# First block, layer 1: tokens kept in the order of their phases from the normalized rows on

## The chip, the cores and the metric

The kernel runs on one core of a Trainium2 chip. The metric is device time in microseconds (us) of one launch, the median of several runs. A core has TensorE (PE in the profile; PEld is its loading of stationary operands, "weight loads" below), VectorE (DVE), ScalarE (ACT), GpSimd (POOL) and SyncE (SP), which in this kernel issues nearly all the transfers (DMAs). Each engine works through its own instructions in order and waits for others by semaphores.

## What is computed

Two transformer-like blocks stand one after the other, each of two layers, on 512 tokens of 1024 features. The change touches only layer 1 of the first block, a dilated attention with six heads of 128 features and three groups:

```
DIL_GROUPS = ((128, 1), (512, 4), (2048, 16))      # (window, dilation)
...
for g, (window, dil) in enumerate(DIL_GROUPS):
    qkv = (h @ w_in[:, base:base + 3 * MIXER_WIDTH]).reshape(B, T, 3, DIL_HEADS, DIL_HEAD_DIM)
    q = partial_rope(qkv[:, :, 0], pos)
    k = partial_rope(qkv[:, :, 1], pos)
    o, lse = dilated_group(q, k, qkv[:, :, 2], window, dil)
```

With dilation 4 a token attends only to tokens of the same remainder by four, its phase; with dilation 16 to those of the same remainder by sixteen, which lie in the same phase too. Group 0 (dilation 1) needs neighbours of all phases. The outputs of the groups are mixed by a softmax over their log-sum-exps; an attention to a small memory, a gate, and `x + branch @ w_out` follow.

## The kernel before

All of `x`, features and weights are 4-byte numbers. A dense product is made exact enough by splitting both operands in two parts, hi and lo, and adding three products (hi hi, hi lo, lo hi). The normalized tokens stand feature-major in the two tiles `hTh` and `hTl`, [128 features, 8, 512 tokens].

`wsplit` (L269) brings a weight unit: a DMA of 512 KB (384 KB for units 384 wide) into `raw` (2 buffers), ACT copies it to `hi`, DVE writes `lo` (4 buffers each). `mm_a_g` (L293) makes a product with features on the partitions: the weights are stationary, 512 tokens stream, 24 products to a unit. `mm_b_g` (L314) makes tokens by features: 128 tokens are stationary, the weight unit streams, 24 products to a token tile.

Layer 0 ends in `w_out` (L714): for each of 4 token tiles 48 products, DVE adds the residual, `pre` (L1794) stores x to DRAM (`xd`) and normalizes, `post` transposes on PE and calls `norm_post` (L365): half of the features at a time, four transposes into `tp` (2 buffers in PSUM), four scalings into `hf`, by turns on ACT and DVE, then `split_into` (L556): ACT writes `hTh`, DVE writes `hTl`. The post of a tile comes a tile later. Before the last post, `fill.step(cols)` emits the first 12312 columns of what follows. In the kernel before that is `dil_values` (L971): the values of three heads, group 0 by token tiles (`v0`, 384 wide, 4 units), then 512 columns (`v1`, 4 units) and 256 columns (`v2`, 2 units) of groups 1 and 2 by phases. `phase_tiles` (L989) takes the stationary tokens of phase p as `xT[..., p::4]`, every fourth element.

`dil_layer` (L992) drains these products, then makes the queries and keys of head 0 (`head`, L1020, six units; `rope_fn` turns 32 rows with DVE, POOL and DVE), and goes through 24 items (6 heads by 4 phases): `front` makes the scores of the three groups in one PSUM tile `at`, `mid` transposes the weights, `back` multiplies by the values; dense products of the next head are stepped in between. In `front` group 0 (L1040) takes `q[:, 128 * a + p:128 * a + 128:4]` as stationary, groups 1 and 2 (L1044) `q[:, p::4]` against `k[:, p::4]`. `mem_stages` (L639) takes the queries `qm` by phases in the same way (L642, 8 fronts of this layer). After head 2 the values of heads 3 to 5 are made by `dil_values` again.

The order of instructions on each engine is set by a scheduler at build time, which goes by priorities and its own costs; weights get a higher priority, so their DMAs come early on SP. In the background `mod_steps` (L417) streams 512-KB rows (`bgraw`) that DVE multiplies (L425, two operations each), one step after so many dense columns.

Of the kernel before, what the change touches and what calls it, by code (L numbers as in the profile page):

```python
# [22 lines left out]
KT = 8  # L23
# [38 lines left out]
def layout(inp):  # L62
    """Rearranges the inputs into the blocks in which the chip reads them."""
# [62 lines left out]
    # the rows of the Fourier features, each beside the row of its mirror  # L126
# [14 lines left out]
def constants():  # L141
# [8 lines left out]
    c["rope1"] = np.stack([np.concatenate([cos, cos]), sn, sn * np.float32(-(128 ** -0.5))], axis=1)  # L150
    m = np.full((128, 4, 512), POS, np.float32)
    q = np.arange(128)
    for p in range(4):
        j = np.arange(256)
# [29 lines left out]
    # along the features 33 cosines and 31 sines (half of them, for the sums with the mirrored tokens); the signs  # L184
    # of a feature under mirroring, and of its mirror's row of weights
# [31 lines left out]
def pipe(items, *stages):  # L217
    """the stages of the items, each a step behind the one before"""
# [7 lines left out]
class Filler:  # L226
    """dense products, emitted a few columns at a time between the steps of a chain"""
# [21 lines left out]
class Builder:  # L249
# [42 lines left out]
    def mm_a_g(self, ps, w, xT, n0, n):  # L292
        """ps[128 features, n tokens] = w.T @ x.T in three passes; yields the columns streamed"""  # L293
# [17 lines left out]
    def mm_b_g(self, ps, xs, units, nk):  # L311
        """ps[128 tokens, n] = x @ w; xs(k) gives the stationary parts; units: [(wh, wl)] of [128, kpu, n]"""
# [36 lines left out]
    def rstd2(self, ss):  # L349
        """the same of a token's two halves"""  # L350
# [14 lines left out]
    def norm_post(self, pool, xn, a, b, dst, sl):  # L365
# [32 lines left out]
    def h_tiles(self, pool, ctx=False):  # L398
        """normed features, feature-major, in two parts: of the tokens, or of the context"""
# [8 lines left out]
    def mod_steps(self, p, todo, bufs):  # L408
        """the parts (layer, which) of the modulation: the conditions' rows times the columns of the weights"""
# [3 lines left out]
        for l, r in todo:  # L413
            # the last layer ends without the context
# [29 lines left out]
    def to_rows(self, row, src, dst):  # L444
        """feature-major columns to rows in DRAM, by way of the tile row"""
# [12 lines left out]
    def tick(self, n):  # L458
        """every so many columns of dense products, one step of the matvecs"""
# [7 lines left out]
    def pool(self, ctx, name, bufs=1, **kw):  # L467
        """a pool of tiles, on the left stack of the memory unless told otherwise"""
# [18 lines left out]
    def small_terms(self):  # L487
        """what hangs on the small inputs alone"""
# [27 lines left out]
        # lower bounds: the first layer's are the cumulative sum less itself, 0  # L516
# [22 lines left out]
        # the 0/1 masks, as the integers a predicated copy wants  # L539
# [448 lines left out]
    def phase_tiles(self, xT):  # L988
        return [(p, lambda k, p=p: (xT[0][:, k, p::4], xT[1][:, k, p::4])) for p in range(4)]  # L989
# [899 lines left out]
```

## Time and profile before

| | |
|---|---|
| median of 3 runs | 2639.84 us (2638.75 to 2646.22) |
| profiled execution, first to last instruction | 2640.8 us |
| PE busy | 2547.6 us (96%) |
| DVE busy | 1518.6 us (58%) |
| ACT busy | 1029.2 us (39%) |
| POOL busy | 174.8 us (7%) |
| mean granted TensorE clock | 0.990 of full speed |
| layer 1 of the first block (about 285 to 785 us) | PE busy 499.2 of 500 us |

A row of a timeline is: start in us, duration in us, engine, line, operation, out<-in, form, count; idle time of the engine and what ended it stand in brackets. In a form such as `128*128 128x256 f32` the first pair is the stationary operand, the second the streaming one. Matmuls are pipelined: their durations overlap, so what one costs on a busy PE is the distance from its start to the next start. Rows of one line, engine or tile give the duration as min/median/max.

### The profile page before, as it was taken

To read this page: it belongs to the slowest core of one execution; us is meant where nothing else is said; L and a number is where in the kernel's file an instruction comes from. 1 tells how busy PE (TensorE), PEld (TensorE's weight loads), DVE (VectorE), ACT (ScalarE), POOL (GpSimd) and SP (SyncE) were. 2 spreads that over 40 slices of the span, in tenths; PEclk is the share of its full clock that TensorE was granted. 3 is DMA by queue.
4 is the path that set the end of the run, shared out by engine and by line. 5 is a ranking of instruction groups with operands and counts; after the bars stand their busy time and mean duration, and the time that the engine had idled before them with its cause. 6 is when DMAs were issued, how large, how long until landed. Compare 5 with 4: busy or idle time off the path is not lost.

```text
span 2640.8 us, 38328 instructions
## 1 busy us (share of the span) xinstructions
PE 2547.6 (96%) x15539; PEld 2125.2 (80%) x15539; DVE 1518.6 (58%) x2502; ACT 1029.2 (39%) x1962; POOL 174.8 (7%) x160
## 2 busy tenths in 40 slices
PE   8999999999999999699999999999999899999998
PEld 7777987797887888577888888888788777888887
DVE  5657678635356467467666644444657676543444
ACT  5523323323345444266642212212655265622222
POOL 0000012102000010010200000000200001000001
PEclk9999999999999999899999999999999999999999
DMA  5424444222132211431544333332221343422222
GB/s 186 153 83 159 158 151 127 89 84 76 45 114 98 73 34 50 141 113 55 199 140 133 127 127 112 120 128 88 80 81 57 103 146 112 139 93 96 96 90 94
DMA packets 85680, 287.24 MB, mean 109 GB/s; under 512 B 9872, under 2 KB 10720, under 8 KB 85120
## 3 DMA queue, kind: packets, MB, share of 16 engines
q1 hardware_dynamic: 85024, 283.42, 32.4%
q8 instruction: 122, 2.00, 0.3%
q10 hardware_dynamic: 480, 1.38, 0.1%
q14 instruction: 54, 0.44, 0.1%
HBM read 257.97 MB, written 25.20 MB: 107 GB/s over the span
## 4 chain that ended last, share of the span: by engine, by line
PE 80%; DMA 5%; DVE 5%; ACT 4%; issue 3%; POOL 1%; SPq 0%; DVEq 0%; POOLq 0%; ACTq 0%
PE acc L302 13%; PE acc L298 13%; PE acc L299 13%; PE acc L318 10%; PE acc L319 10%; PE acc L320 10%; DMA qk0k<-yl 1%; ACT hi L285 1%; PE tp L1399 1%; DVE lo L286 1%; PE at L1044 1%; PE at L1370 1%; DMA raw<-in_wo 1%; PE tp L1392 1%; DMA qk0q<-yl 1%
## 5 line engine op out<-in xcount | busy, mean ns | idle before, releaser
L286 DVE TENSOR_TENSOR lo<-raw,hi 128x1024 fp32r<-128x1024 f32 (+2 forms) x321 | 389.7, 1216 | 415.4 <-ACT hi L285 312.9
L285 ACT ACTIVATE hi<-raw 128x1024 fp32r<-128x1024 f32 (+2 forms) x321 | 335.9, 1048 | 586.7 <-PE acc L299 251.2
L298 PE MATMUL acc<-hTh,hi 128*128 128x512 f32 (+1 forms) x1424 | 554.3, 393 | 2.7 <-ACT hTh L557 2.7
L299 PE MATMUL acc<-hTl,hi 128*128 128x512 f32 (+1 forms) x1424 | 547.1, 388 | 0.3 <-DVE hTl L558 0.2
L302 PE MATMUL acc<-hTh,lo 128*128 128x512 f32 (+1 forms) x1424 | 356.6, 389 | 0.0
L318 PE MATMUL acc<-hi,hTh 128*128 128x512 f32 (+3 forms) x832 | 327.6, 395 | 6.4 <-ACT hi L285 3.7
L319 PE MATMUL acc<-lo,hTh 128*128 128x512 f32 (+3 forms) x832 | 319.2, 384 | 1.7 <-DVE lo L286 1.6
L298 PEld LDWEIGHTS acc<-hTh,hi 128*128 128x128 f32 x1424 | 269.4, 190 | 62.5 <-issue 3.4
L320 PE MATMUL acc<-hi,hTl 128*128 128x512 f32 (+3 forms) x832 | 318.8, 384 | 0.4 <-DVE hTl L558 0.4
L299 PEld LDWEIGHTS acc<-hTl,hi 128*128 128x128 f32 x1424 | 270.1, 190 | 55.0 <-DVE hTl L558 0.7
L302 PEld LDWEIGHTS acc<-hTh,lo 128*128 128x128 f32 x1424 | 258.8, 189 | 56.6
L318 PEld LDWEIGHTS acc<-hi,hTh 128*128 128x128 f32 x832 | 181.3, 218 | 32.8 <-ACT hi L285 6.4
L319 PEld LDWEIGHTS acc<-lo,hTh 128*128 128x128 f32 x832 | 182.4, 219 | 22.5 <-DVE lo L286 5.2
L320 PEld LDWEIGHTS acc<-hi,hTl 128*128 128x128 f32 x832 | 182.0, 219 | 21.9 <-DVE hTl L558 2.7
L318 PE MATMUL acc<-hi,ph 128*128 128x512 f32 x440 | 175.1, 398 | 0.0
L319 PE MATMUL acc<-lo,ph 128*128 128x512 f32 x440 | 174.0, 396 | 0.0
L320 PE MATMUL acc<-hi,pl 128*128 128x512 f32 x440 | 172.7, 393 | 0.0
L298 PE MATMUL acc<-hThc,hi 128*128 128x256 f32 x608 | 150.1, 284 | 0.0
L299 PE MATMUL acc<-hTlc,hi 128*128 128x256 f32 x608 | 148.7, 282 | 0.0
L425 DVE SCALAR_TENSOR_TENSOR bgraw<-bgraw,cb 128x1024 f32<-128x1024 f32 x96 | 117.1, 1219 | 22.0 <-DMA bgraw<-in_w_mod 20.6
L1730 DVE TENSOR_TENSOR y<-y,acc 128x512 f32<-128x512 f32 x112 | 76.4, 684 | 81.1 <-PE acc L320 80.7
L298 PEld LDWEIGHTS acc<-hThc,hi 128*128 128x128 f32 x608 | 115.2, 189 | 2.7
(320 smaller groups left out, 3629.8 us busy)
## 6 DMA issues: line engine op xcount, KB each, us to landing
bgraw<-in_w_mod SPq DMA_DIRECT2D x96, 512.0 KB
raw<-in_wf_in SPq DMA_DIRECT2D x88, 512.0 KB
raw<-in_wf_out SPq DMA_DIRECT2D x44, 512.0 KB
raw<-in_wb_a SPq DMA_DIRECT2D x38, 512.0 KB
raw<-in_wi_a SPq DMA_DIRECT2D x36, 512.0 KB
raw<-in_wo SPq DMA_DIRECT2D x32, 512.0 KB
xt<-xd SPq DMA_DIRECT2D x16, 512.0 KB
raw<-in_wb_v SPq DMA_DIRECT2D x12, 512.0 KB
```

What stands on the lines that cost most here:

```text
L285: nc.scalar.activation(out=hi[:, :n], in_=raw[:, :n], func=AF.Copy)
L286: self.pin = nc.vector.tensor_tensor(out=lo[:, :n], in0=raw[:, :n], in1=hi[:, :n].bitcast(F32), op=ALU.subtract)
L298: mm(ps, lhsT=wh[:, k], rhs=xh[:, k, n0:n0 + n], start=(k == 0), stop=False)
L299: mm(ps, lhsT=wh[:, k], rhs=xl[:, k, n0:n0 + n], start=False, stop=False)
L302: mm(ps, lhsT=wl[:, k], rhs=xh[:, k, n0:n0 + n], start=False, stop=(k == KT - 1))
L318: mm(ps, lhsT=xh, rhs=wh[:, j], start=(k == 0), stop=False)
L319: mm(ps, lhsT=xh, rhs=wl[:, j], start=False, stop=False)
L320: mm(ps, lhsT=xl, rhs=wh[:, j], start=False, stop=(k == nk - 1))
L425: nc.vector.scalar_tensor_tensor(out, raw, 1.0, cb[:, v], ALU.mult, ALU.mult, accum_out=md[:, v, k:k + 1])
L1044: nc.tensor.matmul(ps[:, 128 + 128 * g:256 + 128 * g], lhsT=q[:, p::4], rhs=k[:, p::4], start=True, stop=True)
L1370: nc.tensor.matmul(ps[:, o - k0:o - k0 + n], lhsT=QS[:, 128 * c:128 * c + 128], rhs=KS[:, o:o + n], start=True, stop=True)
L1730: nc.vector.tensor_tensor(out=ys[c][:, hs], in0=ys[c][:, hs], in1=ps, op=ALU.add)
```

## The change

`norm_post` gets an argument `phases`: in layer 1 it writes token m of a tile's phase r to column 128 r + 32 c + m of `hTh` and `hTl` (c: the tile), so the 512 columns stand by phases. It reads `hf` with a step of four elements to do so. From there on every `p::4` becomes a run of 128 neighbours: in the value products and gates (`phase_tiles`), in `front`, in `mem_stages`. The rotation tables and the mask are permuted on the host. Group 0 reads its keys from `kp`, now [128, 4, 160], in eight runs of 32.

Group 0's values are needed by neighbouring tokens: they are made by phase tiles too, copied by ACT into `v0y` (2 buffers), stored by 4 DMAs a tile into a DRAM tile `v0d`, and loaded from there by 4 DMAs in token order. Twice 16 stores of 48 KB and 4 loads of 192 KB.

Since a phase tile needs all four token tiles, the products that are stepped in ahead of the last post are others: `first_units` makes the first two units of head 0 (queries and keys of group 0) in two parts, the columns of the first three token tiles (4 runs of 96 columns) and those of the last one (4 runs of 32), into the two buffers of `at`. The rest of `dil_values` follows in `dil_layer`, with the first product of head 0's third unit ahead of it.

```diff
-            last = self.split_into(hf, dh[:, 4 * kk:4 * kk + 4, sl], dl[:, 4 * kk:4 * kk + 4, sl])
+            if phases is None:
+                last = self.split_into(hf, dh[:, 4 * kk:4 * kk + 4, sl], dl[:, 4 * kk:4 * kk + 4, sl])
+                continue
+            o = slice(32 * phases, 32 * phases + 32)
+            last = self.split_into(hf.rearrange("p j (m r) -> p j r m", r=4),
+                                   *[t[:, 4 * kk:4 * kk + 4].rearrange("p k (r m) -> p k r m", r=4)[:, :, :, o] for t in (dh, dl)])
...
-        yield from self.dense_b_g([(A["wb_v0"][hh, i], (2, 384)) for i in range(4)], self.tok_tiles([(hT, 0, T)]),
-                                  lambda c, ps: nc.scalar.copy(v[0][:, c], ps))
+        d = self.t(self.dr, [4, 4, 32, 384], F32, "v0d")
+
+        def v0(r, ps):
+            y = self.t(vp[0], [128, 384], F32, "v0y", 2)
+            nc.scalar.copy(y, ps)
+            for b in range(4):
+                nc.sync.dma_start(d[b, r], y[32 * b:32 * b + 32])
+
+        yield from self.dense_b_g([(A["wb_v0"][hh, i], (2, 384)) for i in range(4)], self.phase_tiles(hT), v0)
+        for b in range(4):
+            nc.sync.dma_start(v[0][:, b], d[b].rearrange("r m f -> (r m) f"))
...
+    def first_units(self, hT, st):
+        mm = self.nc.tensor.matmul
+
+        def part(sl):
+            n = 4 * (sl.stop - sl.start)
+            xh, xl = [x.rearrange("p k (r m) -> p k r m", r=4)[:, :, :, sl] for x in hT]
+            for u in range(2):
+                if u not in st:
+                    st[u] = self.t(self.ps, [128, 512], F32, "at"), self.wsplit(self.A["wb_a"][u], (KT, 128))
+                ps, (wh, wl) = st[u]
+                o = ps.rearrange("p (r m) -> p r m", r=4)[:, :, sl]
+                for i, (w, x) in enumerate(((wh, xh), (wh, xl), (wl, xh))):
+                    for k in range(KT):
+                        mm(o, lhsT=w[:, k], rhs=x[:, k], start=(i == 0 and k == 0), stop=(i == 2 and k == KT - 1),
+                           skip_group_check=True)
+                        yield n
+                self.tick(3 * KT * n)
+
+        return part(slice(0, 96)), part(slice(96, 128))
+
     def phase_tiles(self, xT):
-        return [(p, lambda k, p=p: (xT[0][:, k, p::4], xT[1][:, k, p::4])) for p in range(4)]
+        return self.tok_tiles([(xT, 0, T)])
...
-                nc.tensor.matmul(ps[32 * a:32 * a + 32, :256], lhsT=q[:, 128 * a + p:128 * a + 128:4],
-                                 rhs=k[:, 128 * a:128 * a + 256], start=True, stop=True, tile_position=(0, 32 * a))
+                nc.tensor.matmul(ps[32 * a:32 * a + 32, :256], lhsT=q[:, 128 * p + 32 * a:128 * p + 32 * a + 32],
+                                 rhs=ap3(k, 32 * a, [[32, 2], [160, 4], [1, 32]]), start=True, stop=True, tile_position=(0, 32 * a))
...
-                nc.tensor.matmul(ps[:, 128 + 128 * g:256 + 128 * g], lhsT=q[:, p::4], rhs=k[:, p::4], start=True, stop=True)
+                nc.tensor.matmul(ps[:, 128 + 128 * g:256 + 128 * g], lhsT=q[:, 128 * p:128 * p + 128], rhs=k[:, 128 * p:128 * p + 128],
+                                 start=True, stop=True)
...
-                 "m": self.mem_stages(l, self.kv[1], qm, os, lambda p: slice(p, None, 4),
+                 "m": self.mem_stages(l, self.kv[1], qm, os, lambda p: slice(128 * p, 128 * p + 128),
...
+        h0 = head(0)
+        next(h0)
         fill.drain()
-        drain(head(0))
+        drain(h0)
...
             vs = {}
+            first = {}
+            fill = Filler(*self.first_units(q["hT"], first))
+            self.w_out(A["wo"][0], brT, res, lambda c: A["x"][128 * c:128 * c + 128], pre, post, fill, 3 * KT * WO_FILL[0])
+            fill.drain()
             fill = Filler(self.dil_values(q["vp"], q["hT"], 0, vs))
-            self.w_out(A["wo"][0], brT, res, lambda c: A["x"][128 * c:128 * c + 128], pre, post, fill, 3 * KT * WO_FILL[0])
```

On PE the order changes in three stretches: after the last products of `w_out` in layer 0, around the value products of heads 0 to 2, and at head 0's own units. Outside them, and in everything after this layer, it stays as it is. At the end of `w_out` PE has, before (`xn_2424` and `xn_2513` are the normalized token tiles 2 and 3, `acc_2564` is value tile 0):

```order
L320 MATMUL acc_2476<-hi_2188,hTl_2061 128x512
L374 MATMUL tp_2515<-ident_69,xn_2424 128x128 x4
L374 MATMUL tp_2527<-ident_69,xn_2424 128x128 x4
L318 MATMUL acc_2564<-hi_2542,hTh_2125 128x384
L319 MATMUL acc_2564<-lo_2543,hTh_2125 128x384
```

In that row 39 products of 384 columns follow before the transposes of tile 3. And now (`at_2539` and `at_2570` are the two first units):

```order
L323 MATMUL acc_2476<-hi_2188,hTl_2061 128x512
L377 MATMUL tp_2515<-ident_69,xn_2424 128x128 x4
L377 MATMUL tp_2527<-ident_69,xn_2424 128x128 x4
L377 MATMUL tp_2586<-ident_69,xn_2513 128x128 x2
L1020 MATMUL at_2539<-hTh_2125,hi_2542 128x4x96 x8
L1020 MATMUL at_2539<-hTl_2126,hi_2542 128x4x96 x8
L1020 MATMUL at_2539<-hTh_2125,lo_2543 128x4x96 x8
L1020 MATMUL at_2570<-hTh_2125,hi_2573 128x4x96 x8
L1020 MATMUL at_2570<-hTl_2126,hi_2573 128x4x96
L377 MATMUL tp_2586<-ident_69,xn_2513 128x128 x2
L377 MATMUL tp_2598<-ident_69,xn_2513 128x128 x4
L1020 MATMUL at_2570<-hTl_2126,hi_2573 128x4x96 x7
```

What came right behind tile 2's transposes needed token tile 0 alone; what comes there now needs tile 2 itself, and two transposes of tile 3 stand ahead of it.

On SP, around the value products, before:

```order
L278 DMA raw_2738<-in_wb_v 128x1024
L278 DMA raw_2744<-in_wb_v 128x1024
L278 DMA raw_2878<-in_wb_v 128x1024
L278 DMA raw_2884<-in_wb_v 128x1024
L421 DMA bgraw_2871<-in_w_mod 128x1024
```

These four are the last two units of `v1` and the two of `v2`. Now (`raw_2911` and `raw_2917` are the same last two units of `v1`):

```order
L281 DMA raw_2905<-in_wb_v 128x1024
L996 DMA v0d_2724<-v0y_2779 32x384 x3
L429 DMA bgraw_2882<-in_w_mod 128x1024
L996 DMA v0d_2724<-v0y_2779 32x384
L996 DMA v0d_2724<-v0y_2810 32x384
L429 DMA bgraw_2975<-in_w_mod 128x1024
L281 DMA raw_2911<-in_wb_v 128x1024
L281 DMA raw_2917<-in_wb_v 128x1024
```

Weight loads now stand behind stores that wait for ACT's copy of a value tile.

## Rows read from the trace of the kernel before

**Rows 1.** Page, part 1: engine, busy us, share of the span, instructions.

```profile
PE 2547.6 (96%) x15539; PEld 2125.2 (80%) x15539; DVE 1518.6 (58%) x2502; ACT 1029.2 (39%) x1962; POOL 174.8 (7%) x160
```

**Rows 2.** Windows: stretch, length, busy of PE, PEld, DVE, ACT, POOL; clock; DMA.

```profile
425.00:545.00 120.00, 120.00 (x756) 97.71 (x754) 76.56 (x134) 36.70 (x64) 19.93 (x13) 1.00 0.30 95
```

**Rows 3.** Timeline of PE, value products v2 of both halves; weight loads there by tile.

```profile
326.45 0.40 PE L320 MATMUL acc<-hi,hTl 128*128 128x256 f32 x1
...
347.22 0.40 PE L319 MATMUL acc<-lo,hTh 128*128 128x256 f32 x1
...
566.68 0.40 PE L318 MATMUL acc<-hi,hTh 128*128 128x256 f32 x1
...
L318 PEld LDWEIGHTS acc<-hi,hTh x22: 329/329/329, 330.1 to 344.8; 128*128 128x128 f32 x22
```

**Rows 4.** Timeline of PE, products of the same shape in the second block.

```profile
1012.80 0.28 PE L318 MATMUL acc<-hi,hThc 128*128 128x256 f32 x1
...
1014.69 0.28 PE L319 MATMUL acc<-lo,hThc 128*128 128x256 f32 x1
```

**Rows 5.** Timeline of PE: a front with the dense products behind it; a back.

```profile
415.85 1.30 PE L1044 MATMUL at<-k,q 128*128 128x128 f32 x4
416.81 0.57 PE L298 MATMUL acc<-hTh,hi 128*128 128x512 f32 x1
417.22 0.39 PE L299 MATMUL acc<-hTl,hi 128*128 128x512 f32 x1
...
419.56 0.39 PE L299 MATMUL acc<-hTl,hi 128*128 128x512 f32 x1
...
423.71 0.71 PE L1070 MATMUL tp<-v,pT 128*128 128x128 f32 x4
424.35 0.67 PE L1040 MATMUL at<-kp,q 128*32 128x256 f32 x8
```

**Rows 6.** Line L642, scores against the memory: in layer 0, then in layer 1.

```profile
L642 PE MATMUL at<-mk,qm x32: 376/376/481, 96.6 to 149.5; 64*128 64x256 f32 x32
...
L642 PE MATMUL at<-mk,qm x32: 394/395/603, 710.4 to 759.5; 64*128 64x256 f32 x32
```

**Rows 7.** Timeline of PE from the last transposes of w_out on.

```profile
284.28 1.03 PE L374 MATMUL tp<-ident,xn 128*128 128x128 f32 x8
285.07 0.42 PE L318 MATMUL acc<-hi,hTh 128*128 128x384 f32 x1
...
292.04 1.04 PE L374 MATMUL tp<-ident,xn 128*128 128x128 f32 x8
...
302.98 0.45 PE L318 MATMUL acc<-hi,hTh 128*128 128x512 f32 x1
```

**Rows 8.** Timeline of DVE, then of ACT, in the same stretch.

```profile
283.10 0.96 DVE L286 TENSOR_TENSOR lo<-raw,hi 128x768 fp32r<-128x768 f32 x1 [0.66 <-ACT hi L285]
...
286.39 0.68 DVE L727 TENSOR_TENSOR res<-res,acc 128x512 f32<-128x512 f32 x1
...
289.40 0.15 DVE L355 SCALAR_TENSOR_TENSOR rv<-ss,rv 128x1 f32<-128x1 f32 x1
...
291.95 1.16 ACT L557 ACTIVATE hTh<-hf 128x512 fp32r<-128x512 f32 x2
```

**Rows 9.** Line L557 on tile hTh: window 250 to 300, then 785 to 850.

```profile
L557 ACT ACTIVATE hTh<-hf x8: 614/633/642, 264.6 to 296.7; 128x512 fp32r<-128x512 f32 x8
...
L557 ACT ACTIVATE hTh<-hf x8: 1098/1120/1151, 814.1 to 847.6; 128x512 fp32r<-128x512 f32 x8
```

**Rows 10.** PE late in the second block: timeline, then windows (length, busy, clock, DMA).

```profile
2258.18 0.63 PE L298 MATMUL acc<-hTh,hi 128*128 128x256 f32 x3 [2.74 <-ACT hTh L557]
...
2258.00:2260.00 2.00, 1.72 (x8) 0.67 0.65 231
2260.00:2262.00 2.00, 2.00 (x11) 0.50 0.07 16
```

**Rows 11.** Chain that ended last, in order of time: a weight load that was waited for.

```profile
784.08 7.04 DMA raw<-in_wo
```

More of the change, by code (lines that the diff above doesn't have):

```diff
@@ L149, in constants @@
     sn = np.concatenate([-sin, sin])
-    c["rope1"] = np.stack([np.concatenate([cos, cos]), sn, sn * np.float32(-(128 ** -0.5))], axis=1)
+    by_phase = np.arange(T).reshape(128, 4).T.reshape(-1)
+    c["rope1"] = np.stack([np.concatenate([cos, cos]), sn, sn * np.float32(-(128 ** -0.5))], axis=1)[:, :, by_phase]
     m = np.full((128, 4, 512), POS, np.float32)
@@ L153, in constants @@
     for p in range(4):
-        j = np.arange(256)
+        j = np.arange(256).reshape(2, 32, 4).transpose(0, 2, 1).reshape(-1)
         a = q[:, None] // 32
@@ L363, in norm_pre, with norm_post @@
         return xn
-    def norm_post(self, pool, xn, a, b, dst, sl):
+    def norm_post(self, pool, xn, a, b, dst, sl, phases=None):
         nc = self.nc
@@ L986, in dil_values, with dil_layer @@
                                   lambda p, ps: nc.scalar.copy(v[2][:, p, 128:], ps))
+    def first_units(self, hT, st):
[15 more added lines that the diff above has]
+        return part(slice(0, 96)), part(slice(96, 128))
     def phase_tiles(self, xT):
-        return [(p, lambda k, p=p: (xT[0][:, k, p::4], xT[1][:, k, p::4])) for p in range(4)]
-    def dil_layer(self, hp, hT, vp, vs, fill, res, before):
+        return self.tok_tiles([(xT, 0, T)])
+    def dil_layer(self, hp, hT, vp, vs, first, fill, res, before):
         nc, tc, A = self.nc, self.tc, self.A
@@ L1000, in dil_layer @@
         os = [self.t(res, [128, 1024], F32, "res") for _ in range(4)]
-        kp = [self.t(l, [128, 640], F32, f"kp{i}") for i in range(2)]
+        kp = [self.t(l, [128, 4, 160], F32, f"kp{i}") for i in range(2)]
         for k in kp:
-            nc.gpsimd.memset(k[:, :128], 0.0)
+            nc.gpsimd.memset(k[:, :, :32], 0.0)
         seg = [(hT, 0, T)]
@@ L1008, in fn @@
             def fn(ps, o, n):
+                ro = [rope[:, i] for i in range(3)]
+                if len(dst.shape) == 3:
+                    ps, *ro = [x.rearrange("p (r m) -> p r m", r=4) for x in (ps, *ro)]
                 if q:
@@ L1013, in fn @@
                 sh = self.t(l, [32, 512], F32, "sh", 2)
+                if len(dst.shape) == 3:
+                    sh = sh.rearrange("p (r m) -> p r m", r=4)
                 nc.vector.stream_shuffle(sh, ps[0:32], [(i + 16) % 32 for i in range(32)])
-                nc.gpsimd.tensor_tensor(out=sh, in0=sh, in1=rope[:, 2 if q else 1], op=ALU.mult)
-                nc.vector.tensor_tensor(out=dst[0:32], in0=dst[0:32], in1=rope[:, 0], op=ALU.mult)
+                nc.gpsimd.tensor_tensor(out=sh, in0=sh, in1=ro[2 if q else 1], op=ALU.mult)
+                nc.vector.tensor_tensor(out=dst[0:32], in0=dst[0:32], in1=ro[0], op=ALU.mult)
                 nc.vector.tensor_tensor(out=dst[0:32], in0=dst[0:32], in1=sh, op=ALU.add)
@@ L1023, in head @@
                 q = self.t(l, [128, 512], F32, f"q{g}", 2)
+                if h == g == 0:
+                    k = kp[0]
+                    for u, f in enumerate((rope_fn(q, True), rope_fn(k[:, :, 32:], False))):
+                        f(first[u][0], 0, T)
+                    qk[h].append((q, k))
+                    continue
                 yield from self.dense_s_g(A["wb_a"][6 * h + 2 * g], seg, rope_fn(q, True))
@@ L1026, in head @@
                     k = kp[h % 2]
-                    yield from self.dense_s_g(A["wb_a"][6 * h + 1], seg, rope_fn(k[:, 128:], False))
+                    yield from self.dense_s_g(A["wb_a"][6 * h + 1], seg, rope_fn(k[:, :, 32:], False))
                 else:
@@ L1847, in post @@
                 self.norm_post(q["np"], xn, *self.norm_vecs(0, 0, 0), q["h"], slice(p, None, 4))
-            brT = self.dil_layer(q["hb"], q["hT"], q["vp"], vs, fill, res, before)
+            brT = self.dil_layer(q["hb"], q["hT"], q["vp"], vs, first, fill, res, before)
             vt, fill = self.scan_values(0, q["vx"], self.segs(q["h"], q["hc"]))
```

2 lines of the change are left out of this document (1 added, 1 removed).

## The prediction

> **What bounds the kernel now.** I began with the page's table of busy times: PE is busy for 2547.6 us [rows 1] of the span of 2640.8. Then windows: through layer 1 of the first block PE is busy for all of a stretch of 120 us at a granted clock of 1.00, while DVE has 76.56 us and ACT 36.70 [rows 2]. So this layer ends when PE is through with its instructions, and only what a PE instruction costs, or an idle PE, moves the end. A busy PE says nothing of its pace; for that I read the timeline from start to start. Where a fourth element of the tokens is the stationary operand, a product of 256 columns takes (347.22 - 326.45) / 89 = 0.233 us, and in the second half, from 566.68 on, the same products stand. Its weight loads show 329 ns [rows 3]. A product of the same shape with contiguous stationary tokens takes (1014.69 - 1012.80) / 16 = 0.118 us [rows 4]. The first is the time of a product of 512 columns, (419.56 - 417.22) / 10 = 0.234 [rows 5]. I read this as a strided load of about 0.233 us, which hides under 512 streamed columns and not under fewer.
>
> **The gains.** Values `v2`: each half has 4 tiles of 24 products of 256 columns, 96, so 192 x (0.233 - 0.118) = 22.1 us. `v1` and the gates stream 512 columns at 0.234 and win nothing, since the load was hidden.
>
> Fronts: the four strided products of L1044 take 416.81 - 415.85 = 0.96 us, and the dense product behind them is followed after 0.41 instead of 0.234. Four contiguous ones of the same shape (L1070) take 0.64 [rows 5]. That is 0.32 + 0.17 = 0.49 for a front, 24 x 0.49 = 11.8 us; the 0.17 is the less certain part, so the low end is 24 x 0.32 = 7.7. The keys of group 0, now in runs of 32, are streamed and not loaded; I take nothing for them.
>
> Memory fronts: 395 against 376 ns [rows 6], 32 x 0.019 = 0.6 us. Sum of the gains: 34.5 us, 30.4 to 36.
>
> The Trainium skill ("TensorE: Matmul & The Clock Gate", LDWEIGHTS) gives a load as its columns over 1.2, 107 ns for 128, whatever the step: by that the step costs nothing and the gains are none in place of 34.5, the last rival below. The trace disagrees, with 0.233 us and 329 ns [rows 3], and I go by the trace.
>
> **The losses.** All but the last lie at the end of layer 0, where the last products of `w_out` are followed by the first of this layer.
>
> *Idle before the first unit.* Before, 39 products behind tile 2's transposes needed token tile 0 alone, from 285.07 to 292.04, and covered the chain from tile 2's transposes to its split [rows 7]. Now the first product needs tile 2's split. That chain, on DVE and ACT: the second `lo` ends at 284.06; the residual add came at 286.39, behind two operations of the modulation (2.33 us), and `hTh` began at 291.95, 5.56 after the add, with two more such operations between the add and `rv` (287.07 to 289.40, 2.33) [rows 8]. In the order of now, the add follows the second `lo` and neither pair stands in the chain: add at 284.8 (it waits for the last product), `hTh` at 284.8 + 5.56 - 2.33 = 288.0. The split reads with a step of four elements; one written with that step took 1120 ns against 633 [rows 9], so I take 1.1 us: the first product at 289.5 with what a semaphore costs. PE is through with the transposes at 285.1 and has nothing else: 4.4 us idle. Bounds: 2.7, as in the one place where PE waits for a split of normalized tokens [rows 10], and 6, if the add stays behind its pair.
>
> *The clock.* After that wait of 2.74 us the granted clock was 0.67 and then 0.50, its lower level of 1.2 GHz, for at least 3 us [rows 10]. The same would cost some 3.4 us at half speed, that is 1.7 lost. Bounds 0 and 2.5.
>
> *Wait ahead of the second part.* Tile 3's last transposes stand ahead of 15 products of 384 columns, each (292.04 - 285.07) / 39 = 0.179 [rows 7], so 2.6 us cover its scalings and its split of 1.1. I take 1.0, bounds 0 and 2.
>
> *The cut itself.* Two units had 48 products of 512 columns at 0.234. Now they are 48 of 384 at 0.178 and 48 of 128. What a short one takes, with a contiguous weight of 128 columns to load, no row shows. The nearest is a transposition of 128 columns, 0.79 / 8 = 0.10 [rows 7]; half of 0.118 is 0.06, and if a load decides as in rows 3 it is 0.234. With 0.10: 48 x (0.178 + 0.10 - 0.234) = 2.1 us; ends 0.2 and 8.5. The result goes to PSUM in 4 pieces; no row shows that, and I take nothing in the middle. The Trainium skill ("PSUM — Partial Sum Buffer", Specifications (TRN2)) says that any non-contiguous pattern there slows matmuls much; that speaks against this change and is part of a rival below. No run here shows it yet.
>
> *Values of group 0.* As many products, of 384 columns, which now load contiguous phase tiles; the way through DRAM delays `v0` until all four tiles are stored, and its first reader is the first `back`, behind `v1`, `v2` and head 0's six units (over 60 us at 0.234): hidden. What it costs if that cover is gone: a store and a load, two transfers of the kind of rows 11. On SP, weight loads now stand behind stores that wait for ACT's copies. ACT has 36.70 of 120 us to do, so a copy comes soon after its tile; PE waits for a late unit or split at the seams. I take 2, bounds 0 and 4 (half of a load of 7.04 [rows 11]).
>
> **Sum.** Losses 4.4 + 1.7 + 1.0 + 2.1 + 2 = 11.2, ends 2.9 and 23. Net 34.5 - 11.2 = 23.3 us less: span 2617.5. The profiled execution of 2640.8 lies 1.0 above the median 2639.84, so I predict 2617. From 785 us on nothing is moved on any engine, and I expect the same times there, only earlier.
>
> **Rivals.**
>
> *The cut is dear.* If a short product takes 0.234, the loss is 6.4 more: 2623. If writing in four pieces doubles both kinds, as a strided load doubled a product in rows 3, the cut costs 48 x (0.356 + 0.20 - 0.234) = 15.5 instead of 2.1: 2630. For it: no row shows such writes. Against it: the runs are 96 and 32 elements long. (By the page on PSUM named above this is what happens.)
>
> *Weights late in `v2`.* A `v2` unit of 512 KB now serves 48 x 0.118 = 5.7 us of products where it served 11.2. If a unit comes only every 7.04 us [rows 11], the two halves cost 4 x 1.4 = 5.6 more: 2623. Against it: head products use a unit of the same size in 24 x 0.234 = 5.6 us, and PE didn't wait for them [rows 2].
>
> *No wait, no clock loss.* The add comes early, the split is quicker than 1.1, the clock stays at its upper level: the losses come down to 3 to 6, 2607 to 2612.
>
> *Slower: SP held up by the stores.* SP works in order. If each of its stores waits for a copy that waits for the products of that tile, the up to 8 units behind them are asked for late; the first two `v1` units cover 11.2 us, of which a load takes 7.04, so it decides from a store's wait of over 4.2 us on. A value tile takes 24 x 0.179 = 4.3 us, so this is near. With 8 loads each 4.3 us late PE loses up to 34: 2651. Against it: between the stores loads are issued, two at a time, and the scheduler's order has only one or two stores between them.
>
> *The step isn't the cause.* If 0.233 has another reason (the pieces of weights, two halves of a tile), then products stay as they are, and the losses stand alone: 2640.8 + 11.2 - 1 = 2651. Against it: the same line with the same shape takes 0.118 [rows 4], and L1044 against L1070 shows the same [rows 5].
>
> **How the numbers follow.** Forecast 0.62; dear cut 0.12 (0.04 of it the doubled writes); late weights 0.08; no wait 0.10; SP 0.05; not the step 0.03. The best sum is 2640.8 - 36 + 2.9 - 1 = 2607. The worst is 2640.8 - 30.4 + 23 - 1 = 2632, and it holds the dear cut and the late weights too. So 2607 to 2632, with about 0.13 outside, most of it above. A measurement of this kernel can tell some 0.3% from no change, 7.9 us: faster means under 2631.9. Forecast, the quick case, the late weights and nearly all of the dear cut are that: 0.88 with a little off for several mishaps at once, which end within 0.3%: 0.05; slower 0.07, the last two rivals without a share that ends within.
>
> **What the changed kernel's profile would show.** `v2` from start to start 0.118, its weight loads well under 329 ns; L1044 from its first row to the next line 0.64 and the product behind it followed after 0.234. Ahead of the first row of L1020 an idle time of 4.4 us ended by `hTh`, then a clock of 0.50; between starts in the second part about 0.10. In the stretch of the value products PE nearly without idle time, and SP's queue without waits of over 4 us. From the last front on the same durations as before, with one shift of about 23 us.
>
> It would be wrong if the short products or those written in pieces take 0.23 or more, if PE waits in the value products for `hi`, or if `v2` stays at 0.233.

## The result and the profile of the changed kernel

The changed kernel takes 2612.02 us in the median (2610.64 to 2620.70, 4 runs) against 2639.99 (2638.75 to 2646.22, 4 runs): 28.0 us less, a ratio of 0.9891 with an interval of 0.987 to 0.9912. Forecast were 2617 us, that is 22.8 less, and a range of 2607 to 2632. In a second set of runs the changed kernel had 2613.11 (0.9893, 0.9878 to 0.9907).

To see where the time went I set the start of an instruction in the trace of after beside that of the same instruction in the trace of before. The last transposes behind layer 0's `w_out` begin 1.48 us earlier (282.80 against 284.28), before anything that was changed; what brings such differences isn't known, and the same transposes begin between 281.99 and 287.62 in the traces below. At the first items of head 0 it is 2.50 us (418.47 against 420.97), at the last steps of the layer 28.89 (755.74 against 784.63). So the layer gained 27.4 us, and of these only 1.0 in its first 135 us.

**The gains.** The timeline of PE of after in `v2`, then its weight loads in that tile (min/median/max of the duration in ns), answers to [rows 3]:

```profile
353.63 0.28 PE L321 MATMUL acc<-hi,hTh 128*128 128x256 f32 x1
...
365.03 0.28 PE L323 MATMUL acc<-hi,hTl 128*128 128x256 f32 x1
L321 PEld LDWEIGHTS acc<-hi,hTh x29: 186/187/188, 353.9 to 364.0; 128*128 128x128 f32 x29
```

95 steps in 11.40 us are 0.120 each, as in [rows 4], and a load shows 187 ns where it showed 329. The same 95 steps took 22.05 us before, so both halves together won 2 x 10.65 = 21.3.

A front of after, as in [rows 5], with the dense products behind it:

```profile
413.37 0.64 PE L1091 MATMUL at<-kp,q 128*32 128x256 f32 x8
413.94 0.71 PE L1095 MATMUL at<-k,q 128*128 128x128 f32 x4
414.41 0.48 PE L301 MATMUL acc<-hTh,hi 128*128 128x512 f32 x1
414.72 0.40 PE L302 MATMUL acc<-hTl,hi 128*128 128x512 f32 x1
```

The four products take 0.47 in place of 0.96, the dense product behind them is followed after 0.31 in place of 0.41, and the eight of group 0 ahead of them take 0.57 in place of 0.60: 0.62 for a front, 14.8 for 24.

A memory front, first of before and then of after:

```profile
710.41 1.31 PE L642 MATMUL at<-mk,qm 64*128 64x256 f32 x4
...
712.11 0.41 PE L319 MATMUL acc<-lo,hTh 128*128 128x512 f32 x1
```

```profile
685.54 1.13 PE L650 MATMUL at<-mk,qm 64*128 64x256 f32 x4
...
686.93 0.40 PE L322 MATMUL acc<-lo,hTh 128*128 128x512 f32 x1
```

One dense product stands between the two rows. From start to start 1.70 became 1.39: 0.31 for each of 8, 2.5 us.

The gates won as well. They take 128 tokens of a phase as stationary and stream 512 columns. Where one stands right behind transposes, here of attention weights (L676, now L684), first of before and then of after:

```profile
706.78 0.60 PE L318 MATMUL acc<-hi,hTh 128*128 128x512 f32 x1
707.22 0.41 PE L319 MATMUL acc<-lo,hTh 128*128 128x512 f32 x1
```

```profile
682.05 0.48 PE L321 MATMUL acc<-hi,hTh 128*128 128x512 f32 x1
682.36 0.40 PE L322 MATMUL acc<-lo,hTh 128*128 128x512 f32 x1
```

It was followed after 0.44 us and is now followed after 0.31 to 0.32. Of the layer's gate products 13 stand so behind transposes or other short products, 1.5 us. The gains found are 40.1 us together. The layer's 27.4 would then leave 12.7 for the losses, which the rows below put at 13.7: 1.0 us of gain stays without a name.

**The losses.** The timeline of PE of after behind layer 0 (it answers to [rows 7]), and the granted clock there (windows: length, busy of PE, PEld, DVE, ACT, POOL; clock; DMA):

```profile
282.80 1.03 PE L377 MATMUL tp<-ident,xn 128*128 128x128 f32 x8
287.75 0.44 PE L377 MATMUL tp<-ident,xn 128*128 128x128 f32 x2 [3.92 <-DVE hf L382]
288.90 2.93 PE L1020 MATMUL at<-hTh,hi 128*128 128x384 f32 x8 [0.71 <-ACT hTh L565]
...
293.36 1.58 PE L1020 MATMUL at<-hTh,lo 128*128 128x384 f32 x8
294.78 1.58 PE L1020 MATMUL at<-hTh,hi 128*128 128x384 f32 x8
...
300.57 0.66 PE L1020 MATMUL at<-hTh,hi 128*128 128x128 f32 x4 [0.33 <-ACT hTh L565]
301.07 1.28 PE L1020 MATMUL at<-hTl,hi 128*128 128x128 f32 x8
302.18 1.06 PE L1020 MATMUL at<-hTh,lo 128*128 128x128 f32 x8
303.08 1.06 PE L1020 MATMUL at<-hTh,hi 128*128 128x128 f32 x8
...
305.76 0.45 PE L301 MATMUL acc<-hTh,hi 128*128 128x512 f32 x1
```

```profile
290.00:292.00 2.00, 2.00 (x8) 2.00 (x8) 0.99 (x1) 0.00 (x0) 0.00 (x0) 0.50 0.99 276
```

From the transposes to the product of L301 lie 22.96 us. Undisturbed and uncut the same work is 16 x 0.099 + 48 x 0.234 = 12.8, so 10.2 are lost here. Idle: 3.92 + 0.71 ahead of the first part, 0.33 in the second. The clock: at 0.50 the first 16 products take 4.46 us in place of 16 x 0.1775 = 2.84, so 1.6. The cut: (294.78 - 293.36) / 8 = 0.1775 for a product of 384 columns, (305.76 - 301.07) / 40 = 0.117 for one of 128, so 48 x (0.1775 + 0.117 - 0.234) = 2.9. Nine and a half of the 10.2 are so named; the rest lies in the ends of what ran just ahead of the three waits.

Waits of PE from there to the end of the layer, after (306 to 755 us) and then before (to 784 us; waiter, what it waited for: us in total, times, longest):

```profile
PE at L1095 <- DVE k L1062: 2.5, 2, 1.5
PE acc L322 <- DVE lo L289: 1.2, 2, 0.6
...
PE acc L321 <- ACT hi L288: 0.3, 1, 0.3
```

```profile
PE at L1044 <- DVE k L1017: 0.4, 1, 0.4
```

PE waits 1.4 us (0.63, 0.28 and 0.54) for `hi` and `lo` among the values, and 2.5 (0.4 before) in the middle of fronts, for keys whose rotation isn't done. The losses are 10.2 + 1.4 + 2.1 = 13.7. That the first of these two kinds comes from the values' new way and the second from the faster `v2` was a guess at this point; two experiments below go after it.

### The profile page after: what moved, and what is told of

Read it like the earlier page. It is cut to its first block, busy times and chain, and to the rows that moved or that the text cites. A ratio compares the mean times of both kernels' runs of the same rounds, so it can differ in the third digit from the quotient of the medians.

```text
span 2608.9 us, 38490 instructions
## 1 busy us (share of the span) xinstructions
PE 2511.9 (96%) x15587; PEld 2073.8 (79%) x15587; DVE 1519.1 (58%) x2502; ACT 1031.9 (40%) x1962; POOL 177.8 (7%) x160
## 4 chain that ended last, share of the span: by engine, by line
PE 76%; DVE 7%; DMA 5%; ACT 5%; issue 4%; POOL 2%; SPq 0%; DVEq 0%; POOLq 0%; ACTq 0%
PE acc L305 13%; PE acc L301 12%; PE acc L302 12%; PE acc L321 9%; PE acc L323 9%; PE acc L322 9%; DVE lo L289 2%; ACT hi L288 1%; DMA qk0k<-yl 1%; PE at L1424 1%; PE tp L1453 1%; PE tp L1446 1%; ACT junk L344 1%; DMA qk0q<-yl 1%; PE at L1289 1%
## 5 line engine op out<-in xcount | busy, mean ns | idle before, releaser
L289 DVE TENSOR_TENSOR lo<-raw,hi 128x1024 fp32r<-128x1024 f32 (+1 forms) x321 | 389.7, 1217 | 394.2 <-ACT hi L288 284.3
L288 ACT ACTIVATE hi<-raw 128x1024 fp32r<-128x1024 f32 (+1 forms) x321 | 335.9, 1048 | 581.5 <-PE acc L302 246.8
L301 PE MATMUL acc<-hTh,hi 128*128 128x512 f32 (+1 forms) x1408 | 546.0, 392 | 2.7 <-ACT hTh L565 2.7
L302 PE MATMUL acc<-hTl,hi 128*128 128x512 f32 (+1 forms) x1408 | 540.5, 388 | 0.3 <-DVE hTl L566 0.2
L321 PE MATMUL acc<-hi,hTh 128*128 128x512 f32 (+3 forms) x832 | 316.7, 383 | 5.8 <-ACT hi L288 3.1
L301 PEld LDWEIGHTS acc<-hTh,hi 128*128 128x128 f32 x1408 | 265.8, 189 | 61.3 <-issue 3.6
L322 PE MATMUL acc<-lo,hTh 128*128 128x512 f32 (+3 forms) x832 | 311.0, 375 | 2.8 <-DVE lo L289 2.6
L323 PE MATMUL acc<-hi,hTl 128*128 128x512 f32 (+3 forms) x832 | 311.2, 375 | 0.4 <-DVE hTl L566 0.4
L321 PEld LDWEIGHTS acc<-hi,hTh 128*128 128x128 f32 x832 | 157.1, 189 | 38.6 <-ACT hi L288 7.0
L322 PEld LDWEIGHTS acc<-lo,hTh 128*128 128x128 f32 x832 | 157.5, 189 | 29.1 <-DVE lo L289 7.1
L323 PEld LDWEIGHTS acc<-hi,hTl 128*128 128x128 f32 x832 | 157.3, 189 | 27.4 <-DVE hTl L566 2.7
L301 PE MATMUL acc<-hThc,hi 128*128 128x256 f32 x608 | 150.7, 285 | 0.0
L301 PEld LDWEIGHTS acc<-hThc,hi 128*128 128x128 f32 x608 | 115.9, 191 | 2.6
```

What stands on the lines that cost most here:

```text
L288: nc.scalar.activation(out=hi[:, :n], in_=raw[:, :n], func=AF.Copy)
L289: self.pin = nc.vector.tensor_tensor(out=lo[:, :n], in0=raw[:, :n], in1=hi[:, :n].bitcast(F32), op=ALU.subtract)
L301: mm(ps, lhsT=wh[:, k], rhs=xh[:, k, n0:n0 + n], start=(k == 0), stop=False)
L302: mm(ps, lhsT=wh[:, k], rhs=xl[:, k, n0:n0 + n], start=False, stop=False)
L321: mm(ps, lhsT=xh, rhs=wh[:, j], start=(k == 0), stop=False)
L322: mm(ps, lhsT=xh, rhs=wl[:, j], start=False, stop=False)
```

## Experiments

### Which step costs: stationary or streamed, four or two

```diff
-        yield from self.dense_b_g([... wb_v2 ...], self.phase_tiles(hT),
+        yield from self.dense_b_g([... wb_v2 ...], self.step_tiles(hT, (4, 2)[hh]),
...
-                nc.tensor.matmul(ps[...], lhsT=q[:, 128 * p:128 * p + 128], rhs=k[:, 128 * p:128 * p + 128],
+                run, step = slice(128 * p, 128 * p + 128), slice(p, None, 4)
+                nc.tensor.matmul(ps[...], lhsT=q[:, step if h < 3 else run], rhs=k[:, run if h < 3 else step],
```

> The changed kernel with steps put back, so that other tokens are read: v2 of heads 0 to 2 takes its stationary tokens with a step of four elements, v2 of heads 3 to 5 with a step of two; in the fronts of heads 0 to 2 only the stationary queries of groups 1 and 2 have the step of four, in those of heads 3 to 5 only the streamed keys. My theory, that a step in the stationary operand slows its load: v2 with step four 0.233 us from start to start in place of 0.118 (that stretch 11 us longer), fronts of heads 0 to 2 with 0.96 us for the four products in place of 0.47, fronts of heads 3 to 5 unchanged at 0.47. For step two I expect 0.118, since the Trainium skill (SBUF — State Buffer) has lines of 16 bytes of which two elements are then used; if each skipped element costs, some 0.17. The rival, that the streamed step costs or the two together: fronts of heads 3 to 5 slow, those of heads 0 to 2 quick. Time by my theory: 11 + 12 x 0.6 = 18 us more than the changed kernel, about 2630; by the rival about 2619 to 2630 with the halves the other way round.

The timeline of PE: `v2` of heads 0 to 2 (first and last product), `v2` of heads 3 to 5 (first and last), a front of heads 0 to 2, one of heads 3 to 5:

```profile
355.94 0.29 PE L321 MATMUL acc<-hi,hTh 128*128 128x256 f32 x1
...
377.99 0.40 PE L323 MATMUL acc<-hi,hTl 128*128 128x256 f32 x1
...
576.24 0.28 PE L321 MATMUL acc<-hi,hTh 128*128 128x256 f32 x1
...
587.64 0.28 PE L323 MATMUL acc<-hi,hTl 128*128 128x256 f32 x1
...
456.71 1.20 PE L1103 MATMUL at<-k,q 128*128 128x128 f32 x4
457.67 0.47 PE L301 MATMUL acc<-hTh,hi 128*128 128x512 f32 x1
457.98 0.40 PE L302 MATMUL acc<-hTl,hi 128*128 128x512 f32 x1
...
604.13 1.16 PE L1103 MATMUL at<-k,q 128*128 128x128 f32 x4
604.92 0.59 PE L301 MATMUL acc<-hTh,hi 128*128 128x512 f32 x1
605.35 0.40 PE L302 MATMUL acc<-hTl,hi 128*128 128x512 f32 x1
```

Step four brings back the 22.05 us of 95 steps to the hundredth (0.232 each); step two costs nothing (11.40). So `v2`'s gain is the stationary operand's step of 16 bytes. The Trainium skill (SBUF — State Buffer, Door 1: The DMA port swizzle, its note on lines of 16 bytes) says that two hits on a line are needed for full rate; with elements of 4 bytes step two has two and step four one, and the trace agrees at both: 0.120 and 0.232.

In the fronts I was half wrong. A stepped stationary operand gives 0.96 and no effect on the product behind (0.31). A stepped streamed operand alone, which I had expected at 0.47, gives 0.79, and the product behind is then followed after 0.43. Each of the two alone makes the front slow, and together they are no slower than the stationary one (0.96, then 0.41 [rows 5]). The kernel as a whole had 2634.61 us, one run, against the 2630 expected; the 12 fronts with the streamed step, 0.44 us longer each, would be 5 us, about the difference; runs of one kernel differ by as much, so this one time doesn't show it. PE waited 0.7 us ahead of fronts for rotated keys in this trace, against 2.5.

### The first units not cut, and cut in the middle

The first experiment puts the two first units behind both posts and streams all 512 columns, the second cuts them between token tiles 1 and 2:

```diff
-        return part(slice(0, 96)), part(slice(96, 128))
+        return [part(slice(0, 128))]
...
-            fill = Filler(*self.first_units(q["hT"], first))
+            fill = Filler()
...
-            fill.drain()
+            Filler(*self.first_units(q["hT"], first)).drain()
```

```diff
-WO_FILL = (513, 760)
+WO_FILL = (512, 760)
...
-        return part(slice(0, 96)), part(slice(96, 128))
+        return part(slice(0, 64)), part(slice(64, 128))
```

With 512 the last post comes right behind the 48 products of the first half.

> The changed kernel with the first two units not cut: their products stream all 512 columns, and stand behind the posts of tiles 2 and 3, with nothing ahead of them. Theory (what the cut buys is cover, what it costs is 48 short products): PE idles from the transposes of tile 2 to the split of the first half of tile 3, about 7 to 8 us in place of 5.0, the clock falls likewise (1.6 lost, up to 2.5), and the cut's 3.0 us come back: 0 to 2 us more than the changed kernel, about 2612 to 2614. Rival (the short products or the four pieces in PSUM are what the stretch loses by): 3 to 6 us less than the changed kernel.

> The changed kernel with the first two units cut in the middle: the columns of token tiles 0 and 1 (4 runs of 64), which need neither tile 2 nor 3, then those of tiles 2 and 3. Theory: the wait of 4.6 us for tile 2's split is gone, since 48 x 0.118 = 5.7 us stand there, and the clock stays at 1.00; the two halves cost 48 x (0.118 + 0.118 - 0.234) = 0.1 in place of 3.0; ahead of the second half PE waits 2 to 4 us for tile 3's split, since its transposes come behind the first half. 3 to 7 us less than the changed kernel. Rival (the wait is only moved): the wait for tile 3 is as long as that for tile 2 was, the clock falls there, and only the 3 us of the cut come back.

PE's timeline not cut, then cut in the middle:

```profile
294.04 1.97 PE L377 MATMUL tp<-ident,xn 128*128 128x128 f32 x8 [5.38 <-DVE hf L382]
299.55 3.45 PE L1020 MATMUL at<-hTh,hi 128*128 128x512 f32 x8 [3.54 <-ACT hTh L565]
```

```profile
283.55 1.03 PE L377 MATMUL tp<-ident,xn 128*128 128x128 f32 x8
...
294.06 2.29 PE L1020 MATMUL at<-hTh,hi 128*128 128x256 f32 x9 [2.90 <-ACT hTh L565]
...
300.27 1.11 PE L1020 MATMUL at<-hTh,lo 128*128 128x256 f32 x8
301.22 0.39 PE L301 MATMUL acc<-hTh,hi 128*128 128x512 f32 x1
...
387.05 0.76 PE L1095 MATMUL at<-k,q 128*128 128x128 f32 x2 [5.25 <-DVE k L1062]
```

Of the one cut in the middle, a window behind that last wait, and the first operation of the rotation that was waited for:

```profile
387.00:390.00 3.00, 2.95 (x8) 2.50 (x9) 0.86 (x3) 0.81 (x2) 0.00 (x0) 0.50 0.10 41
```

```profile
383.79 0.71 DVE L1059 STREAM_SHUFFLE sh<-acc 32x512 f32<-32x512 f32 x1
```

Not cut, PE idles 8.9 us, and from the transposes (287.62) to L301 (312.21) it is 24.6, against 23.0 and, in a second trace of the changed kernel, 24.1: the cut saves what it costs and about 1 us more. Cut in the middle it is 17.7: the wait for tile 2 is gone, and 5.3 us are won, inside the 3 to 7 expected, though the clock, which was to stay at 1.00, was at 0.50 from 294 to 296 us. And then the kernel had 2613.63, no better than the changed one. The wait at the first front shows why: 5.25 us, where the changed kernel waited 1.5, and a clock of 0.50 behind it.

The kernel that isn't cut waits 5.7 there and had 2627.43 against the 2612 to 2614 expected. Against the changed kernel its starts are 4.8 us late before the end of layer 0, ahead of anything that was changed, 6.5 at L301, and 12.8 behind the first items. So the local terms came out near what was expected and the sum did not (each kernel was timed once): what is won ahead of the values can be given back at the first front.

What is late there is DVE. In the kernel cut in the middle the last product of the keys' unit is through at 377.4 us, but DVE, which works from 369.9 to 385.1 without a pause (weights, the background, the rotations of other units), begins with these keys at 383.79, 6.3 us later; in the changed kernel it begins at 384.05, 2.1 us behind the unit.

### Group 0's values without the way through DRAM

```diff
-            y = self.t(vp[0], [128, 384], F32, "v0y", 2)
-            nc.scalar.copy(y, ps)
-            for b in range(4):
-                nc.sync.dma_start(d[b, r], y[32 * b:32 * b + 32])
+            nc.scalar.copy(v[0][:, r], ps)
...
-        for b in range(4):
-            nc.sync.dma_start(v[0][:, b], d[b].rearrange("r m f -> (r m) f"))
```

> The changed kernel without the way through DRAM: ACT copies the phase tiles of group 0's values straight into v0, so that these values stand in the order of the phases where the backs expect that of the tokens; no stores and no loads. Theory (the way through DRAM is hidden, and SP isn't held up by it): the time of the changed kernel within 1 us, the waits for hi and lo among the value products unchanged (some 1.4 us). Rival (weight loads late behind the stores are what PE waits for there): these waits gone, 1 to 3 us less.

2612.98, one run. Waits of PE between the first units and the end of the layer (306 to 755 us):

```profile
PE acc L321 <- ACT hi L288: 0.7, 1, 0.7
PE acc L322 <- DVE lo L289: 0.6, 1, 0.6
```

1.3 us for `hi` and `lo` without the stores, 1.4 with them, as the theory said: the waits at the values don't come from the stores, and the way through DRAM is hidden. What brings these waits (units of 5.6 us of products on two `raw` buffers, or an order that needs the units sooner) stays open.

### Three first units, and products ahead of the first front

The first front waits for the rotation of the keys of group 2, the last unit of head 0. Between that unit's last product and the front's second half, the scheduler put 19 products in the changed kernel, 17 in the one cut in the middle; two products are 0.5 us, so most of the longer wait is DVE's. Three kernels follow from this, timed on one chip beside the changed one. The first takes a third unit (the queries of group 1) among the first ones, all cut in the middle, so that 72 products of 256 columns need tiles 0 and 1 alone, with tile 3's transposes among them (`WO_FILL` and the cut as above):

```diff
-            for u in range(2):
+            for u in range(3):
...
+                if h == 0 and g == 1:
+                    rope_fn(q, True)(first[2][0], 0, T)
```

The second leaves the cut alone and puts a unit of head 1 ahead of the first front; the third does both:

```diff
+                if hh == i == 0:
+                    fill.step(24 * 512)
```

> The changed kernel again, as it is, beside the next three on one chip: 2612 within 2 us, 27 to 29 us less than the kernel before.

> The changed kernel with three first units in place of two, each cut in the middle (token tiles 0 and 1, then 2 and 3), tile 3's transposes between the second unit's first half and the third's. Theory of the cut (cover decides): no wait of PE over 0.5 us between the last product of layer 0 and the values, no fall of the clock, no cost of the cut, so the value products begin 8 us earlier against the first transposes than in the changed kernel. Theory of what comes behind (the first front waits for the keys of group 2, whose rotation stands on DVE behind the background operations and the weights' lo, and this gives back what was won ahead of it): 14 products or 3.3 us stand between those keys' last product and the front, so the front waits 2 to 5 us, and 3 to 6 us less than the changed kernel remain. Rival (what the last look gave back was chance, late weights in that one run): 8 us less remain.

> The changed kernel with one unit of head 1 (24 products, 5.6 us) put ahead of the first front. Theory (the front waits for the rotation of keys that have only just been made): the wait of 1.5 us ahead of the front's last two products is gone, 1 to 2 us less than the changed kernel, unless later fronts then lack products to stand beside. Rival (DVE as a whole is late in this stretch, not this one chain): the wait moves to the next front, time unchanged.

> Both edits: three first units cut in the middle, and one unit of head 1 ahead of the first front. Theory: the gain ahead of the values is kept, 7 to 10 us less than the changed kernel, 2602 to 2605. Rival (DVE or the weights bound the stretch from the values to the second item): the front or the products of head 1 wait for what was won, and at most 4 us less remain.

| kernel | median us | ratio to before, interval | transposes to L301, less the added unit | wait at the first front |
|---|---|---|---|---|
| changed kernel again | 2613.11 | 0.9893, 0.9878 to 0.9907 | 24.1 | 1.4 |
| three units | 2608.79 | 0.9875, 0.9860 to 0.9890 | 23.1 - 5.6 = 17.5 | 2.7 |
| a unit ahead of the front | 2618.74 | 0.9909, 0.9894 to 0.9924 | 25.8, with a second fall of the clock | none |
| both | 2605.59 | 0.9857, 0.9841 to 0.9874 | 21.6 - 5.6 = 16.0 | none |

PE's timeline with three units, then with both, and, behind each, a window with the clock just behind the wait for tile 3:

```profile
294.43 0.86 PE L1020 MATMUL at<-hTh,hi 128*128 128x256 f32 x5 [1.98 <-ACT hTh L565]
...
383.37 0.46 PE L1098 MATMUL at<-k,q 128*128 128x128 f32 x2 [2.69 <-DVE k L1062]
```

```profile
296.00:298.00 2.00, 2.00 (x12) 1.88 (x11) 0.52 (x1) 0.17 (x1) 0.00 (x0) 0.61 0.03 8
```

```profile
299.47 0.86 PE L1020 MATMUL at<-hTh,hi 128*128 128x256 f32 x5 [1.86 <-ACT hTh L565]
```

```profile
300.00:302.00 2.00, 1.85 (x14) 1.52 (x14) 1.56 (x2) 0.44 (x1) 0.00 (x0) 1.00 0.05 20
```

With three units the wait for tile 2 is gone as in the kernel cut in the middle; the wait for tile 3 is 2 us where I had expected under 0.5. The first front then waits 2.7 us, inside the 2 to 5 expected, and 4.3 us remain of the gain, inside 3 to 6; the four runs (2607.57 to 2610.19) lie below those of the changed kernel (2611.92 to 2616.00), but the two intervals overlap. With both edits the front doesn't wait (its four products of L1098 stand together at 386.57), and 7.5 us remain: 0.9857 against 0.9893, whose intervals just part. That is the lowest time found. The clock fell behind 2 us of idle time in the one trace and not in the other.

The unit ahead of the front alone was a miss: 5.6 us slower than the changed kernel in the median, not 1 to 2 faster (the intervals overlap, so what is sure is that it isn't better). Its trace has no wait for the keys, but this one, and behind it the clock of the window:

```profile
429.13 1.08 PE L1091 MATMUL at<-kp,q 128*32 128x256 f32 x8 [3.41 <-DVE dmx L1099]
```

```profile
429.00:434.00 5.00, 4.87 (x36) 3.34 (x37) 3.16 (x8) 1.63 (x5) 0.51 (x1) 0.50 0.31 102
```

The 24 products are missing at the end of head 0's items: there two fronts follow each other without a dense product, and the second one waits for DVE to have read the first one's scores. In that profile the clock was low once more from 304.7 to 311.5, 3 us behind a wait of only 0.34 us, which cost another 3 us by the shift of the starts there; a wait of the same length stands there in four other traces with this cut, and the clock stayed up. With both edits the same front waits 0.9 us and the clock doesn't fall there. So in this trace the rival (the wait moves to a later front) was right about the wait, and moving products only pays where the place that gives them can spare them.

### Half a unit, and a fourth unit

```diff
-                    fill.step(24 * 512)
+                    fill.step(12 * 512)
```

```diff
-            for u in range(3):
+            for u in range(4):
...
+                    if h == 0 and g == 1:
+                        rope_fn(k, False)(first[3][0], 0, T)
```

Both edits start from the kernel with both edits of the section above, the second from the first of these.

> Three first units cut in the middle, and half a unit of head 1 (12 products, 2.8 us) ahead of the first front in place of a whole one. Theory (products are moved, not made: what stands ahead of the first front is missing beside the items of head 0 that come last): the front's wait of 2.7 us that the kernel with three units and nothing ahead had falls to under 1, and the later fronts wait no more than in the kernel with a whole unit ahead: 8 to 10 us less than the changed kernel, 1.2 to 1.4% less than the kernel before. Rival (a whole unit is needed to cover the rotation): as with three units alone, 4 us less.

> The same with a fourth unit among the first ones (keys of group 1), cut in the middle too. Theory: another 2.8 us of products that need only tiles 0 and 1 stand ahead of the wait for tile 3's split, so that this wait of 1.9 us and the clock's fall behind it are gone, 2 us less than with three. Rival (weights): four units hold all four pairs of hi and lo until their second halves are through, so the value units of group 0 come late and PE waits 2 to 5 us for hi or lo at their first products; as fast as with three or slower.

2606.97 (0.9870, 0.9855 to 0.9885) and 2607.42 (0.9863, 0.9847 to 0.9880). With half a unit the front waits 2.90 us as with none, since the scheduler again leaves 14 products between the keys' last one and the front's second half: on the wait the rival was right, and a whole unit is needed to cover it. The time doesn't decide: its interval overlaps those of the kernels with three units alone (0.9860 to 0.9890) and with both edits. With four units the wait for tile 3 falls to 0.30 us as my theory said, and PE waits at the values, as the rival said:

```profile
PE acc L321 <- ACT hi L288: 2.4, 1, 2.4
PE acc L322 <- DVE lo L289: 2.3, 2, 2.0
```

At each of the two long ones, 2.4 and 2.0, the clock fell. Neither kernel can be told from the version with both edits.

## Why the prediction came out

The direction, the range and, in the main, the mechanism were right, and the net was 5 us too small (22.8 against 28.0). The gains were put too low (34.5 against 40.1 found, above even the bound of 36, which was given without working), the losses too low as well (11.2 against 13.7, of which 2.1 are a wait that I did not name). That the one error took back a part of the other is luck.

- `v2`: 22.1 forecast, 21.3 measured, and the experiment with steps shows that the stationary step is its cause. The rival that the step isn't it falls. The formula of the Trainium skill for a load (TensorE: Matmul & The Clock Gate, LDWEIGHTS) counts columns alone; the trace disagrees, with 187 and 329 ns for the same 128 columns.
- Fronts: 11.8 forecast, 14.8 measured. The term was mis-sized. I took the new pace from four products of another line, 0.64 [rows 5], and these stand behind a line with other operands; the front itself now takes 0.47. The dense product behind it won 0.10 and not 0.17. I also gave the whole price to the stationary operand; the streamed one has a step that costs as well.
- Memory fronts: 0.6 forecast, 2.5 measured. Mis-sized because I took the difference of two durations [rows 6]. Durations of pipelined products overlap; from start to start it is 0.31 a front, not 4 x 0.019.
- Gates: nothing forecast, since the load was held to be hidden under 512 columns; 1.5 measured, where a gate's product stands behind a transpose or another short product.
- Idle ahead of the first unit: 4.4 forecast, 4.6 measured. The chain worked out from [rows 8] took 1.2 us longer (`hTh` began at 287.74, not at 288.0 less the shift of 1.5), and two transposes of tile 3 filled a part of it. The split took the 1.1 us assumed. The half clock: 1.7 forecast, 1.6 measured, though in the second trace of the same kernel it lasted to 295 and cost more.
- Wait ahead of the second part: 1.0 forecast, 0.3 measured. The cut: 2.1 forecast, 2.9 measured (a short product 0.117, not 0.10). The four pieces in PSUM cost nothing: 0.1775 for 384 columns in 4 runs of 96, against 0.179 in one run [rows 7]. That part of a rival, and the sentence of the Trainium skill on any non-contiguous pattern (PSUM — Partial Sum Buffer), find no support here for runs of 96 or 64 (0.119 a product of 256 columns in 4 runs of 64, (301.22 - 300.27) / 8, against 0.120 in one run).
- Waits at the values: 2 forecast, 1.4 measured; the stores are not their cause.
- What I did not name is the wait at the fronts, 2.5 us where 0.4 stood. In the experiments other edits lose their gain there. That it comes from the faster `v2` is likely but not shown alone: with the steps put back, in `v2` and in the fronts of these heads, it was 0.7.
- SP: its stores waited for ACT's copies four times, 7.4 us in sum and 2.5 at most, under the 4.2 from which the slower rival would have decided; that rival fell.

The 1.0 us between the profiled execution and the median didn't matter: the traces' spans differ by 31.9 us, the layer by 27.4, the medians by 28.0; the rest is the start (1.5) and the second block (3.0), where no instruction was moved.

## What to carry to other kernels

Size a product on a busy TensorE from start to start with the one that follows, never by its duration, and take the pace of an operation from a row with the same line and neighbours. If a stationary or a streamed operand of 4-byte elements has a step of four and its products are short (here 128 and 256 columns; among products of 512 there was next to nothing to win), lay it out in runs at the place where it is written: here that made each of eight splits on ACT 1.1 us long in place of 0.63. And after a gain look at the next wait in the program: the cut in the middle won 5 us and lost them again at the first front, until products were there to cover it.

## What the runs showed of the hardware

- Steps: stationary, four elements 0.232 us and two elements 0.120 for a product of 256 columns; streamed, four elements 0.79 for a front against 0.47. I had expected only the first.
- A product of 128 columns with a new contiguous stationary tile each takes 0.112 (303.08 - 302.18 over 8), hardly less than one of 256 columns, 0.119. It is written in four runs of 32; the four of a front, written in one run each, take 0.47 / 4 = 0.118. Below 256 columns something other than the columns sets the pace here.
- In this layer, over all traces, at each wait of PE of 2.9 to 5.7 us the clock fell to 0.50, within it or just behind it, or was there already; at six waits of 1.8 to 2.7 us it fell three times, and in one trace the clock fell 3 us behind a wait of 0.34 us.
